# A hybrid decoder layer: attention without carried states, another order of the last steps, and eight unread products

## The chip, the cores and the metric

The kernel runs on one core of a Trainium2 chip. The metric is the time on the device in microseconds (us) of one execution, the median of several; less is better. The engines are named as the profile names them: PE is TensorE (PEld its weight loads), DVE is VectorE, ACT is ScalarE, POOL is GpSimd, SP is SyncE, whose queue issues nearly all loads.

## The reference, cut to what matters

One layer over 256 tokens of width 1024: a token mixer (gated linear attention, GLA, with 4 heads, and a short convolution beside it), then a mixture of 64 experts with two experts per token, then a norm. In chunks of 64 tokens the attention is

```python
b = jnp.cumsum(gc, axis=3)                  # gc: log of the forget gate, within a chunk
q_t = qc * jnp.exp(b)
k_t = kc * jnp.exp(-b)
k_s = kc * jnp.exp(b_last - b)
attn = jnp.where(causal, jnp.einsum('nbhid,nbhjd->nbhij', q_t, k_t), 0.0)
o_intra = jnp.einsum('nbhij,nbhjv->nbhiv', attn, vc)
def step(state, inp):                       # over the four chunks
    q_i, k_i, v_i, d_i = inp
    o_i = jnp.einsum('bhid,bhdv->bhiv', q_i, state)
    return d_i[..., None] * state + jnp.einsum('bhid,bhiv->bhdv', k_i, v_i), o_i
o = o_intra + o_inter                       # then a norm per head, silu(r), a projection
```

and the end of the layer

```python
x = x + g2 * hier_moe(h)        # each expert: (silu(x @ w1[e]) * (x @ w3[e])) @ w2[e]
return rmsnorm(x, final_norm_g)
```

Everything is fp32 with 476 MB of weights, most of them the experts'; all 64 experts are computed.

## The kernel before

**Loads.** `Stream` issues the weights from SP's queue. The projections' weights come in blocks of 128x1024 into a ring of 12 slots (`bfree`, L72); a slot is loaded again when `bdone` says that its block is used up. Whatever tiles the first part doesn't need any more become slots for units of 2 MB (128x4096, `free`, L107), 12 units for each of 16 groups of 4 experts. So a load starts when the engine that used the slot's last content is done.

**First part (to about 292 us).** The projection `h @ W_in` and the output projections go through `items`, blocks of 128 output columns (`mm_blk`, L356: 24 products, high and low part of the split fp32 operands). For each block ScalarE rounds the weights (`split_h`, L340) and VectorE takes the remainder (`split_l`, L347), five blocks ahead. VectorE also forms the modulation vectors from weights as they come (`mod_blk`, L257; table `MODS` says beside which block). All else is hung on a block's number: `first(b, f)` runs f ahead of that block's weight casts, `pre(b, f)` ahead of its `split_l`, `at(b, f)` just before its products. The engines work in the order written, so this sets what stands behind what.

**Attention in it.** `gate0` to `gate8` form the forget gate; `gate4` scans it within chunks of 64 (bb). `eb`, `enb` and `ekb` are exp(b), exp(-b), exp(b_last - b); `q_evac` and `k_evac` multiply them into q and k as these leave PSUM (qt, kt_, ks). `gla_kst` (L481) transposes ks, `gla_attn` (L494) forms 128x128 scores per head and half of the tokens, `gla_attn2` (L498) copies their causal part within chunks into `at`. `gla_state` (L506) forms k_s^T v for chunks 0, 1 and 2, `gla_state2` (L513, L515) decays and adds them. `gla_o` sums per head and half of the head's 256 value columns two products with `at` (L525) and three with the states (L529). `gla_ss` to `gla_ss4` form the norms; `gla_ss4` spreads the four rows of `scr2` over 128 partitions by products with the mostly zero `P1` (L556). PSUM tiles `m` come from four banks in turn (`mt`).

**Experts.** Per group of four experts: 8 units of the first layer (`l1_unit`, through `tile_mm`, L1048: four strips of 32 columns), `act` (silu, product, four transposes L1059, copy), 4 units of the second layer, `evac_y` (L1066: output weights into SBUF), and during the next group `combine` (L1075: back to the tokens, L1079: added to `total`).

**The end.** The last group's second layer is stored by output columns (`el`, `LASTC`: 512, 256, 128 and 128 columns), each of its units loaded in `LASTN` pieces. Each part goes through `last_mm` (L1200) and `last_part` (L1066, L1075, L1079, squares on L1214 and, for the last, on L1211); `last_weigh` (L1218) multiplies by the final gain. Then come the sum of squares (L1241), root, reciprocal, scaling and four stores (L1247 to L1252). The order is that of the code:

```python
last_mm(part 0) ; last_part(0)
last_mm(part 1) ; last_weigh(0) ; last_part(1)
last_mm(part 2) ; last_weigh(1) ; last_part(2)
last_mm(part 3) ; last_weigh(2) ; last_part(3, True)
```

Of the kernel before, what the change touches and what calls it, by code (L numbers as in the profile page):

```python
# [28 lines left out]
LASTN = (2, 2, 4, 4)  # L29
# [88 lines left out]
def trunk_kernel(ctx: ExitStack, tc: tile.TileContext, xT: bass.AP, c: bass.AP, modw: bass.AP,  # L118
# [113 lines left out]
    V.memset(cmask[0:64, 64:128], 0)  # L232
# [219 lines left out]
    def gate5():  # L452
        S.activation(eb, bb, AF.Exp, scale=-1.0 / 16)

    def gate6():
        V.tensor_sub(ekb.rearrange("p h (c t) -> p (h c) t", t=64),
                     b4[:, :, 63:64].to_broadcast([128, 16, 64]), b4)

    def gate7():
# [16 lines left out]
    def gla_kst():
        L["pk"] = []
        for tt in range(TT):
            ps = mt(H, 128)
            for h in range(H):  # L480
                T.transpose(ps[:, h], ks[:, h, 128 * tt:128 * tt + 128], ident)  # L481
            L["pk"].append(ps)

    def gla_kst2():
        for tt in range(TT):
            S.copy(L["kst"][:, tt], fl(L["pk"][tt]))

    def gla_attn():
        L["pa"] = []
        for tt in range(TT):  # L490
            s = slice(128 * tt, 128 * tt + 128)
            ps = mt(H, 128)
            for h in range(H):
                T.matmul(ps[:, h], kt_[:, h, s], qt[:, h, s], start=True, stop=True)  # L494
# [2 lines left out]
    def gla_attn2(tt):
        V.copy_predicated(L["at"][:, tt], cmask[:, None, :].to_broadcast([128, H, 128]), L["pa"][tt])  # L498

    def gla_state(*chs):  # L500
        for ch in chs:
            L["ps", ch] = [mt(2, 256) for _ in range(2)]
        for h in range(H):
            for ch in chs:
                tt, r = ch // 2, slice(64 * (ch % 2), 64 * (ch % 2) + 64)
                T.matmul(L["ps", ch][h // 2][:, h % 2], L["kst"][r, tt, 128 * h:128 * h + 128],  # L506
                         L["v"][r, tt, 256 * h:256 * h + 256], start=True, stop=True)

    def gla_state2(ch):
        new = L["S", ch + 1]  # L510
        for h in range(H):
            if ch == 0:
                S.copy(new[:, h], L["ps", ch][h // 2][:, h % 2])  # L513
            else:
                V.scalar_tensor_tensor(new[:, h], L["S", ch][:, h], decay[:, h, ch:ch + 1],  # L515
                                       L["ps", ch][h // 2][:, h % 2], op0=OP.mult, op1=OP.add)

    def gla_o(h):
        ps = mt(2, TOK)
        vt = L["v"]  # L520
        for a in range(2):
            f = 256 * h + 128 * a
            for tt in range(TT):
                s = slice(128 * tt, 128 * tt + 128)
                T.matmul(ps[:, a, s], vt[:, tt, f:f + 128], L["at"][:, tt, h],  # L525
                         start=(a == 0 and tt == 0), stop=False, skip_group_check=True)
            for ch in range(1, 4):
                s = slice(64 * ch, 64 * ch + 64)
                T.matmul(ps[:, a, s], L["S", ch][:, h, 128 * a:128 * a + 128], qt[:, h, s],  # L529
                         start=False, stop=(a == 1 and ch == 3), skip_group_check=True)  # L530
# [20 lines left out]
    def gla_ss4():  # L551
        L["rso"] = []
        for h in range(H):
            if h % 2 == 0:
# [1 line left out]
            T.matmul(L["rso"][h // 2][:, h % 2], P1[:, h // 2, h % 2], scr2, start=True, stop=True)  # L556
# [764 lines left out]
```

## Time and profile before

| what | value |
|---|---|
| time, median of 3 runs | 1206.16 us (1203.33 to 1206.17) |
| the profiled execution, its own time | 1202.4 us |
| its span in the profile | 1200.5 us |
| PE busy | 903.8 us (75%) |
| DVE busy | 381.6 us (32%) |
| ACT busy | 224.6 us (19%) |
| read from memory | 475.79 MB, 397 GB/s over the span |

The span is counted from the first to the last recorded event; the time of the execution is 1.9 us more. A busy share is a mean over stages that differ: the share of the whole says little about which engine another waits for at a given time. In the timeline a row is a start, a length, the engine, the code's line, the operation, the tile written and the tiles read, the size, a count, and in brackets the idle time ahead of it with what ended it.

### The profile page before, as it was taken

The page shows a single profiled execution, that of the slowest core. Times are in us where ns is not written, and L with a number is a line of the kernel's source. Part 1 is how long each engine was busy: PE and PEld are TensorE (multiplying, and loading weights), DVE is VectorE, ACT ScalarE, POOL GpSimd, SP SyncE. Part 2 cuts the span into 40 slices and gives each one's busy share as a digit, 9 for nine tenths or more (in the row PEclk, how much of TensorE's full clock was granted, in tenths as well). Part 3 has the DMA queues.
Part 4 walks back from the last instruction along what each step waited for, and adds up shares of the span by engine and source line. Part 5 has one row for each costly group of instructions (what it writes and reads, how often), then busy time and mean ns, then how long its engine had stood idle before and what let it go on. Part 6 is the DMA issues. An engine that isn't in the chain of part 4 may idle for free.

```text
span 1200.5 us, 14607 instructions
## 1 busy us (share of the span) xinstructions
PE 903.8 (75%) x6188; PEld 476.8 (40%) x6188; DVE 381.6 (32%) x720; ACT 224.6 (19%) x375; POOL 3.9 (0%) x15
## 2 busy tenths in 40 slices
PE   9999999999888766666666667676667566756575
PEld 6999999999342212121212212121212111412112
DVE  8968699664431111111111101020202000302103
ACT  6775545443210101010101000000000000100002
POOL 0000000000000000000000000000000000000000
PEclk9999999999998888798788888788888886989888
DMA  9987589979999999999999999999999999999996
GB/s 369 396 339 254 177 300 339 381 271 364 421 430 430 429 432 431 430 431 430 430 432 430 429 432 430 430 432 429 431 431 430 431 430 431 428 432 431 429 428 261
DMA packets 51483, 477.84 MB, mean 398 GB/s; under 512 B 5971, under 2 KB 6099, under 8 KB 27093
## 3 DMA queue, kind: packets, MB, share of 16 engines
q1 hardware_dynamic: 50544, 475.81, 95.8%
q8 instruction: 50, 0.82, 0.2%
q10 hardware_dynamic: 868, 1.05, 0.2%
q14 instruction: 21, 0.16, 0.0%
HBM read 475.79 MB, written 1.05 MB: 397 GB/s over the span
## 4 chain that ended last, share of the span: by engine, by line
DMA 67%; PE 28%; DVE 3%; ACT 0%; issue 0%; DVEq 0%; SPq 0%; ACTq 0%
DMA unit<-in_ew_dram 45%; DMA ring<-in_ew_dram 19%; PE z L356 17%; PE a L1048 3%; DMA unit<-in_el_dram 2%; PE m L364 2%; PE z L373 2%; PE m L1020 1%; PE m L1075 1%; PE m L529 0%; DMA xt<-in_xT_dram 0%; PE z L220 0%; PE m L506 0%; PE m L525 0%; PE m L312 0%
## 5 line engine op out<-in xcount | busy, mean ns | idle before, releaser
L1048 PE MATMUL a<-unit,xt 128*32 128x512 f32 x1440 | 209.5, 711 | 103.9 <-DMA unit<-in_ew_dram 103.9
L1048 PE MATMUL a<-unit,gt 128*32 128x512 f32 x736 | 121.7, 799 | 63.5 <-DMA unit<-in_ew_dram 59.9
L1048 PEld LDWEIGHTS a<-unit,xt 128*32 128x32 f32 x1440 | 43.8, 120 | 248.2 <-DMA unit<-in_ew_dram 139.0
L356 PE MATMUL z<-hhl,sp 128*128 128x256 f32 x1152 | 140.9, 284 | 0.0
L356 PEld LDWEIGHTS z<-hhl,sp 128*128 128x128 f32 x1152 | 138.9, 192 | 1.6 <-issue 1.5
L1024 ACT ACTIVATE xt<-m,modc,A 128x128 f32<-128x128 f32 x64 | 25.9, 453 | 518.5 <-PE m L1020 517.4
L347 DVE TENSOR_TENSOR sp<-ring,sp 128x1024 fp32r<-128x1024 f32 x88 | 106.8, 1219 | 40.2 <-ACT sp L340 40.1
L1048 PE MATMUL a<-ring,xt 128*32 128x512 f32 x608 | 84.2, 676 | 35.9 <-DMA ring<-in_ew_dram 35.9
L340 ACT CAST sp<-ring 128x1024 fp32r<-128x1024 f32 x88 | 91.5, 1048 | 93.8 <-PE z L356 66.6
L1079 DVE TENSOR_TENSOR wk<-wk,m 128x512 f32<-128x512 f32 (+2 forms) x64 | 41.7, 654 | 194.5 <-PE m L1075 194.5
L1066 DVE TENSOR_TENSOR xt<-a,xt 128x1024 f32<-128x1024 f32 (+3 forms) x19 | 20.0, 1054 | 257.4 <-PE a L1048 249.8
L1048 PEld LDWEIGHTS a<-unit,gt 128*32 128x32 f32 x736 | 24.3, 129 | 148.6 <-DMA unit<-in_ew_dram 93.1
L1075 PE MATMUL m<-xt,pwt 128*128 128x512 f32 (+2 forms) x136 | 64.5, 617 | 5.2 <-DVE xt L1066 5.2
L1056 DVE TENSOR_TENSOR gt<-gt,a 128x512 f32<-128x512 f32 x16 | 11.0, 687 | 173.8 <-ACT gt L1055 173.8
L1020 PEld LDWEIGHTS m<-scr,wk 128*128 128x128 f32 x512 | 58.7, 192 | 19.0 <-issue 18.7
L1020 PE MATMUL m<-scr,wk 128*128 128x128 f32 x512 | 62.4, 279 | 3.7 <-DVE scr L1009 2.9
L257 DVE SCALAR_TENSOR_TENSOR xt<-ring,xt 128x1024 f32<-128x1024 f32 x48 | 58.5, 1218 | 0.6 <-DMA ring<-in_modw_dram 0.2
L1048 PEld LDWEIGHTS a<-ring,xt 128*32 128x32 f32 x608 | 18.6, 117 | 97.3 <-DMA ring<-in_ew_dram 49.3
L1026 DVE TENSOR_SCALAR xt<-m,A,modc 128x128 f32<-128x128 f32 x64 | 23.3, 405 | 103.9 <-PE m L1020 103.9
L1048 PE MATMUL a<-ring,gt 128*32 128x512 f32 x208 | 36.3, 833 | 21.8 <-DMA ring<-in_ew_dram 21.1
L1075 PEld LDWEIGHTS m<-xt,pwt 128*128 128x128 f32 x136 | 26.0, 206 | 50.3 <-issue 38.0
L1055 ACT ACTIVATE gt<-a 128x512 f32<-128x512 f32 x16 | 9.6, 597 | 182.3 <-PE a L1048 182.3
(255 smaller groups left out, 633.0 us busy)
## 6 DMA issues: line engine op xcount, KB each, us to landing
unit<-in_ew_dram SPq DMA_DIRECT2D x136, 2048.0 KB, 38.8
ring<-in_ew_dram SPq DMA_DIRECT2D x48, 2048.0 KB, 38.8
ring<-in_win_dram SPq DMA_DIRECT2D x88, 512.0 KB, 7.8
ring<-in_modw_dram SPq DMA_DIRECT2D x48, 512.0 KB, 6.8
ring<-in_ew_dram SPq DMA_DIRECT2D x12, 512.0 KB, 7.3
unit<-in_el_dram SPq DMA_DIRECT2D x4, 1024.0 KB, 31.6
ring<-in_el_dram SPq DMA_DIRECT2D x4, 512.0 KB, 20.2
unit<-in_el_dram SPq DMA_DIRECT2D x4, 512.0 KB, 11.2
```

The source lines that it names most:

```text
L257: V.scalar_tensor_tensor(scr, st.block("m", i, b), 1.0, cB, op0=OP.mult, op1=OP.mult, accum_out=modc[:, 4 * i + b:4 * i + b + 1])
L340: S.copy(sp(b)[:, 0], st.block("w", n, i))
L347: V.tensor_sub(t[:, 1], st.block("w", n, i), t[:, 0].bitcast(F32))
L356: T.matmul(ps, t[:, ws, k], rhs[rs][:, k], start=(clear and k == 0 and n == 0), stop=(k == KT - 1 and n == 2), skip_group_check=True)
L364: T.matmul(pb[:, h % 2], t[:, ws, h], hl[rs][:, kk], start=(kk == 0 and h % 2 == 0 and n == 0), stop=(kk == KT - 1 and h % 2 == 1 and n == ...
L373: T.matmul(pv[tt][hh], hl[rs][:, kk, 128 * tt:128 * tt + 128], t[:, ws, 512 * hh:512 * hh + 512], start=(kk == 0 and n == 0), stop=(kk == ...
L1020: T.matmul(ps[j], acc[:, tt, f:f + 128], Pm[:, tt], start=(tt == 0), stop=(tt == 1))
L1024: S.activation(xg[:, k], ps[j], AF.Identity, bias=B2[:, k:k + 1], scale=A2[:, k:k + 1])
L1026: V.tensor_scalar(xg[:, k], ps[j], A2[:, k:k + 1], B2[:, k:k + 1], op0=OP.mult, op1=OP.add)
L1048: T.matmul(ps[32 * j:32 * j + 32, 512 * hh:512 * hh + 512], lhsT[:, 32 * j:32 * j + 32], w[:, j, 512 * hh:512 * hh + 512], start=first, st ...
L1075: T.matmul(ps[:, :w], pwt[:, tt], X["y"][:, s], start=True, stop=True)
L1079: V.tensor_add(total[:, tt, s], total[:, tt, s], ps[:, :w])
```

## The change

Three edits go together. Lines called L... in the rows below are of the kernel that the rows are of.

**1. Attention without states.** A half of 128 tokens is now scaled about its own middle: for keys, `ek` holds in a half's first chunk the decay from the token to that chunk's end (from `wE`), and in its second chunk the inverse of the decay since that chunk's start; for queries, `eq` is 1/`ek`. So a key times a later query of the same half has the decay between them, and needs no state (`kx`, `qx`). For the second half's queries against the first half's keys `gla_far` multiplies the keys by the decay over the second chunk and the queries by that over the third (`decay`; `kd`, `qd`). `gla_attn` forms near scores (128 columns for the first 64 keys, 64 for the other 64) and far ones, `gla_near` copies the causal part, `gla_cross` the far part, and `gla_o` needs two products per head and half: one over all 256 tokens, one over the last 128. `gla_kst`, `gla_state` and their evacuations are gone. `gla_ss4` spreads the norm rows with one row of ones each (K of 1, partitions 0, 32, 64, 96) into four PSUM tiles, so P1 need not be cleared. Three blocks of `MODS` change places.

**2. Another order at the end.** `last_part` is cut into `last_evac` and `last_sums`; part 3's products follow part 2's at once, parts 2 and 3 lie in another PSUM tile (`ps2`), the gains are multiplied in smaller steps, the final scaling of the last 256 columns takes the gain along, and five stores take the place of four. `LASTN` goes from (2, 2, 4, 4) to (1, 2, 2, 4).

**3. Unread products.** In the last group five products of ones (bf16, 512 columns) into a PSUM tile that nothing reads stand between the units u = 6 and u = 7 of the first layer (called unit 6 and unit 7 below), and three more ahead of the silu's transposes.

TensorE's order in the attention before (`z` are the projections' blocks, `m` the attention's PSUM tiles; the counts are the code's):

```order
L356 MATMUL z<-hhl,sp 128x256 x240
L481 MATMUL m<-ident,gb 128x128 x8
L356 MATMUL z<-hhl,sp 128x256 x24
L494 MATMUL m<-gb 128x128 x8
L356 MATMUL z<-hhl,sp 128x256 x24
L506 MATMUL m<-t_126,gc 128x256 x8
L356 MATMUL z<-hhl,sp 128x256 x48
L506 MATMUL m<-t_126,gc 128x256 x4
L356 MATMUL z<-hhl,sp 128x256 x48
L525 MATMUL m<-gc,t_126 128x128 x2
L529 MATMUL m<-gb,gc 128x64 x3
```

and after:

```order
L352 MATMUL z<-hhl,sp 128x256 x288
L487 MATMUL m<-gb 64x128
L488 MATMUL m<-gb 64x64
...
L485 MATMUL m<-gb 128x128 x4
L352 MATMUL z<-hhl,sp 128x256 x96
L505 MATMUL m<-gc,t_120 128x256
L506 MATMUL m<-gc,t_120 128x128
```

Transposes and states are gone; near scores (L487, L488, eight pairs) and far ones (L485) stand together, one block later than the scores before, and an output needs two products for five.

ScalarE's order at the gate's exponentials (`t_181`, `t_175` and `gb` are the gate tiles, L340 and L336 the casts for the splits) before:

```order
L340 CAST sp<-ring 128x1024
L453 ACT_TABLE_LOAD
L453 ACTIVATE t_181<-t_181 128x1024
L340 CAST sp<-ring 128x1024
L715 COPY t_126<-z 128x512
L463 ACTIVATE t_181<-t_181 128x1024
L464 ACTIVATE gb<-gb 128x1024
L340 CAST sp<-ring 128x1024 x2
L715 COPY t_126<-z 128x512
```

and after:

```order
L336 CAST sp<-ring 128x1024
L460 ACT_TABLE_LOAD
L460 ACTIVATE t_175<-gb 128x8x64
L461 ACTIVATE t_175<-t_175 128x8x64
L460 ACTIVATE t_175<-gb 128x8x64
L461 ACTIVATE t_175<-t_175 128x8x64
L463 ACTIVATE decay<-t_175 128x4 x2
L336 CAST sp<-ring 128x1024
L684 COPY t_120<-z 128x512
L336 CAST sp<-ring 128x1024 x2
L684 COPY t_120<-z 128x512
```

The one exponential ahead of the cast is now four of half the size and two of four columns; the two that stood behind the next copy are gone.

TensorE's order at the end before (L1048 the last group's first layer, L1200 the second layer's parts, L1075 the combining):

```order
L1048 MATMUL a<-unit,xt 32x512 x24
L1059 MATMUL m<-ident,gt 128x128 x4
L1200 MATMUL a<-unit,gt 32x512 x16
L1075 MATMUL m<-xt,pwt 128x512 x2
L1200 MATMUL a<-ring,gt 32x256 x16
L1075 MATMUL m<-xt,pwt 128x256 x2
L1200 MATMUL a<-unit,gt 32x128 x16
L1075 MATMUL m<-xt,pwt 128x128 x2
L1200 MATMUL a<-unit,gt 32x128 x16
L1075 MATMUL m<-xt,pwt 128x128 x2
```

and after, from unit 7 of the first layer on (L1016 is the first layer, L1182 the second, L1051 the combining; five unread products stand ahead of the first row):

```order
L1016 MATMUL a<-unit,xt 32x512 x8
L1026 LDWEIGHTS onesb
L1026 MATMUL m<-onesb 128x512
...
L1026 MATMUL m<-onesb 128x512
L1035 MATMUL m<-ident,gt 128x128 x4
L1182 MATMUL a<-unit,gt 32x512 x16
L1051 MATMUL m<-xt,pwt 128x512 x2
L1182 MATMUL a<-ring,gt 32x256 x16
L1051 MATMUL m<-xt,pwt 128x256 x2
L1182 MATMUL a<-unit,gt 32x128 x32
L1051 MATMUL m<-xt,pwt 128x128 x4
```

Three unread products stand ahead of the transposes, part 3's products have joined part 2's, and both are combined after them. In VectorE's order the evacuations of both (`last_evac`) accordingly stand ahead of the last four additions.

The diff, cut:

```diff
-LASTN = (2, 2, 4, 4)
+LASTN = (1, 2, 2, 4)
...
-MODS = (16, 17, 18, 19, 22, 26, 27, 28, 31, 33, ...
+MODS = (16, 17, 18, 19, 22, 26, 28, 29, 30, 33, ...
...
-    V.memset(cmask[0:64, 64:128], 0)
...
-    G.memset(P1, 0.0)
-    for h in range(H):
-        G.memset(P1[32 * h:32 * h + 1, h // 2, h % 2], 1.0)
...
+    wE, qx, kx = gb[:, 0, 0:2].rearrange("p h t -> p (h t)"), gb[:, 1], gb[:, 3]
...
+    def half(t, c):
+        return t.rearrange("p h (a c t) -> p (h a) c t", c=2, t=64)[:, :, c]
...
     def gate5():
-        S.activation(eb, bb, AF.Exp, scale=-1.0 / 16)
+        V.tensor_sub(wE, half(bb, 0)[:, :, 63:64].to_broadcast([128, 8, 64]), half(bb, 0))
     def gate6():
-        V.tensor_sub(ekb.rearrange("p h (c t) -> p (h c) t", t=64),
-                     b4[:, :, 63:64].to_broadcast([128, 16, 64]), b4)
-    def gate7():
-        V.tensor_copy(decay, eb.rearrange("p h (c t) -> p h c t", t=64)[:, :, :, 63])
-    def gate8():
-        S.activation(enb, bb, AF.Exp, scale=1.0 / 16)
-        S.activation(ekb, ekb, AF.Exp, scale=-1.0 / 16)
+        for d, sg in ((ek, -1.0), (eq, 1.0)):
+            S.activation(half(d, 0), wE, AF.Exp, scale=sg / 16)
+            S.activation(half(d, 1), half(bb, 1), AF.Exp, scale=-sg / 16)
+        for c in range(2):
+            S.activation(decay[:, c], bb[:, :, 64 * c + 127], AF.Exp, scale=-1.0 / 16)
...
+    def gla_far():
+        for d, x, c, o in ((kd, kx, 0, 0), (qd, qx, 1, 128)):
+            V.tensor_mul(d, x[:, :, o:o + 128], decay[:, c, :, None].to_broadcast([128, H, 128]))
...
     def gla_attn():
         L["pa"] = []
-        for tt in range(TT):
-            s = slice(128 * tt, 128 * tt + 128)
+        a, b = slice(0, 128), slice(128, 256)
+        for k, q in ((kx[:, :, a], qx[:, :, a]), (kx[:, :, b], qx[:, :, b]), (kd, qd)):
             ps = mt(H, 128)
             for h in range(H):
-                T.matmul(ps[:, h], kt_[:, h, s], qt[:, h, s], start=True, stop=True)
+                if k is kd:
+                    T.matmul(ps[:, h], k[:, h], q[:, h], start=True, stop=True)
+                    continue
+                T.matmul(ps[0:64, h], k[:, h, 0:64], q[:, h], ...)
+                T.matmul(ps[64:128, h, 64:128], k[:, h, 64:128], q[:, h, 64:128], ...)
             L["pa"].append(ps)
...
+    def gla_near(tt):
+        t, ps = (L["at0"][:, :, 0:128], L["at1"])[tt], L["pa"][tt]
+        for n, c in ((64, 0), (128, 64)):
+            V.copy_predicated(t[:n, :, c:c + 64], cmask[:n, None, c:c + 64]..., ps[:n, :, c:c + 64])
+    def gla_cross():
+        S.copy(L["at0"][:, :, 128:256], L["pa"][2])
     def gla_o(h):
...
+            T.matmul(ps[:, a], vt[:, 0, f:f + 128], L["at0"][:, h], start=(a == 0), ...)
+            T.matmul(ps[:, a, 128:256], vt[:, 1, f:f + 128], L["at1"][:, h], ...)
...
     def gla_ss4():
-        L["rso"] = []
+        L["rso"] = [mt(TOK) for _ in range(H)]
         for h in range(H):
-            if h % 2 == 0:
-                L["rso"].append(mt(2, TOK))
-            T.matmul(L["rso"][h // 2][:, h % 2], P1[:, h // 2, h % 2], scr2, start=True, stop=True)
+            r = slice(32 * h, 32 * h + 1)
+            T.matmul(L["rso"][h], onesf[r], scr2[r], start=True, stop=True)
...
-    at(21, gate6)
-    first(22, gate5)
-    first(23, gate8)
-    at(23, gate7)
+    at(21, gate5)
+    first(22, gate6)
...
+    at(27, gla_far)
-    at(27, gla_kst)
-    at(28, gla_attn)
-    first(28, gla_kst2)
-    pre(29, gla_attn2, 0)
-    pre(29, gla_attn2, 1)
-    at(29, gla_state, 0, 1)
-    first(30, gla_state2, 0)
-    pre(30, gla_state2, 1)
-    at(31, gla_state, 2)
-    pre(32, gla_state2, 2)
+    at(29, gla_attn)
+    first(31, gla_cross)
+    pre(31, gla_near, 0)
+    pre(31, gla_near, 1)
...
     def k_evac(j):
-        V.tensor_mul(ks[:, s], pk[j], ekb[:, s])
-        V.tensor_mul(kt_[:, s], pk[j], enb[:, s])
+        V.tensor_mul(kx[:, s], pk[j], ek[:, s])
...
+    def unread(n):
+        p = mt()
+        for _ in range(n):
+            T.matmul(p, onesb, onesb[:, None, :].to_broadcast([128, 4, 128]), start=True, stop=True)
-    def act(ps):
+    def act(ps, fill=0):
+        if fill:
+            unread(fill)
         S.activation(gt, ps[:, 0:512], AF.Silu)
...
             l1_unit(ps, g, u, unit("e", g, u))
+            if g == last and u == 6:
+                unread(5)
...
-        act(ps)
+        act(ps, 3 if g == last else 0)
...
-    last_weigh(0)
-    last_part(1)
+    last_evac(1)
+    last_weigh(0, 512, 0, 1)
+    last_sums(1)
+    last_weigh(0, 512, 1, 2)
...
-    for f in range(4):
-        last_mm(768, 128, w[:, 0, f], f)
-    last_weigh(1)
-    last_part(2)
-    for f in range(4):
-        last_mm(896, 128, w[:, 1, f], f)
-    last_weigh(2)
-    last_part(3, True)
+    for n in (2, 3):
+        for f in range(4):
+            last_mm(n, w[:, n - 2, f], f)
+        if n == 2:
+            last_evac(2)
+    last_weigh(512, 256)
+    last_evac(3)
+    last_sums(2)
+    last_sums(3)
...
+    put(V, nc.sync, 0, 0, 512)
+    put(S, S, 1, 0, 512)
+    put(V, nc.sync, 0, 512, 1024)
+    put(S, S, 1, 512, 768)
+    put(V, nc.sync, 1, 768, 1024)
```

More of the change, by code (lines that the diff above doesn't have):

```diff
@@ L411, in trunk_kernel @@
     L["o"] = gb[:, 2:4].rearrange("p a h t -> p (a h) t")
-    ekb, qt, kt_, ks = (gb[:, i] for i in range(4))
-    decay = sm.tile([128, H, 4], F32, name="decay")
-    b4 = bb.rearrange("p h (c t) -> p (h c) t", t=64)
+    wE, qx, kx = gb[:, 0, 0:2].rearrange("p h t -> p (h t)"), gb[:, 1], gb[:, 3]
+    wE = wE.rearrange("p (a t) -> p a t", t=64)
+    kd, qd = (gb[:, 2].rearrange("p h t -> p (h t)")[:, 512 * i:512 * i + 512].rearrange("p (h t) -> p h t", h=H)
+              for i in range(2))
+    decay = sm.tile([128, 4, H], F32, name="decay")
+    def half(t, c):
+        return t.rearrange("p h (a c t) -> p (h a) c t", c=2, t=64)[:, :, c]
     def gate0():
@@ L497, in gla_attn2 @@
[L497 to L507, printed above, removed]
@@ L522, in gla_o @@
             f = 256 * h + 128 * a
[L523 to L530, printed above, removed]
+            T.matmul(ps[:, a], vt[:, 0, f:f + 128], L["at0"][:, h], start=(a == 0), stop=False, skip_group_check=True)
+            T.matmul(ps[:, a, 128:256], vt[:, 1, f:f + 128], L["at1"][:, h], start=False, stop=(a == 1),
+                     skip_group_check=True)
         L["po", h] = ps
@@ L1195, in trunk_kernel, with last_mm, last_evac, last_sums @@
     S.activation(dum, epsc, AF.Sqrt)
-    def last_mm(c0, cw, w, f):
+    ps2 = pa.tile([128, D], F32, name="a")
+    LASTP = (ps[:, 0:512], ps[:, 512:768], ps2[:, 0:128], ps2[:, 512:640])
+    sq1 = X["xg"][(last + 1) % 2].rearrange("p k s -> p (k s)")
+    def last_mm(n, w, f):
         for j in range(EPG):
-            T.matmul(ps[32 * j:32 * j + 32, c0:c0 + cw], gT[:, f, 32 * j:32 * j + 32], w[:, j],
+            T.matmul(LASTP[n][32 * j:32 * j + 32], gT[:, f, 32 * j:32 * j + 32], w[:, j],
                      start=(f == 0), stop=(f == 3), skip_group_check=True)
-    def last_part(n, tail=False):
+    def last_evac(n):
+        s = slice(LASTC[n][0], sum(LASTC[n]))
+        V.tensor_mul(X["y"][:, s], LASTP[n], X["g2r"][:, s])
+    def last_sums(n):
         c0, cw = LASTC[n]
-        evac_y(ps, c0, c0 + cw)
         combine(last, c0, c0 + cw)
@@ L1248, in trunk_kernel, with put @@
[L1248 to L1252 removed]
+    def put(e, q, tt, c0, c1):
+        t, r = total[:, tt, c0:c1], rs[:, tt:tt + 1]
+        if e is S:
+            S.activation(t, t, AF.Copy, scale=r)
+        elif c0 == 768:
+            V.scalar_tensor_tensor(t, t, r, fgr[:, c0:c1], op0=OP.mult, op1=OP.mult)
+        else:
+            V.tensor_scalar(t, t, r, None, op0=OP.mult)
+        q.dma_start(out[128 * tt:128 * tt + 128, c0:c1], t)
```

70 lines of the change are left out of this document (24 added, 46 removed).

## The prediction

> **What bounds the kernel now.** I read the page's slices first, then the busy time in stretches of 10 us, then the chain of waits, and last the timeline where the change stands. What the DMA moved in each slice of 30 us, and the chain's shares by engine:
>
> ```profile
> GB/s 369 396 339 254 177 300 339 381 271 364 421 430 430 429 432 431 430 431 430 430 432 430 429 432 430 430 432 429 431 431 430 431 430 431 428 432 431 429 428 261
> ...
> DMA 67%; PE 28%; DVE 3%; ACT 0%; issue 0%; DVEq 0%; SPq 0%; ACTq 0%
> ```
>
> From the twelfth slice on the DMA moves about 430 GB/s without a break: the expert weights. Before that it falls as low as 177. The stretches tell why (busy us of TensorE, its weight load, VectorE, ScalarE, GpSimd, with counts; granted clock; DMA share; GB/s):
>
> ```profile
> 120.00:130.00 10.00, 10.00 (x90) 10.00 (x89) 4.07 (x6) 4.26 (x6) 0.00 (x0) 1.00 0.51 161
> ...
> 310.00:320.00 10.00, 10.00 (x92) 3.46 (x88) 3.12 (x16) 5.12 (x13) 0.00 (x0) 1.00 1.01 429
> ```
>
> At 120 us TensorE (PE) is busy for the whole stretch and the DMA for half of it: buffers come free only as fast as TensorE uses them up. At 310 us it is the DMA that is full. The chain of waits (start, length, what) joins the two:
>
> ```profile
> 368.88 5.38 PE a L1048 x32
> 374.28 37.96 DMA unit<-in_ew_dram
> ...
> 1179.98 1.11 PE a L1200 x8
> ```
>
> So there are three stages. Up to 374.28 us the chain is mostly TensorE; from there the stream of weights runs for its own length, until 1179.98; then a ladder of short steps ends the program. A microsecond saved on TensorE in the first stage frees each later buffer a microsecond earlier and moves the whole stream. Engine time saved between 374 and 1180 us is worth nothing. The ladder counts one for one.
>
> **The attention: what goes.** TensorE's timeline of before (start, length; an fp32 product is recorded as two passes, so counts are twice the code's):
>
> ```profile
> 94.59 1.04 PE L481 MATMUL m<-ident,gb 128*128 128x128 f32 x8
> 95.38 3.11 PE L356 MATMUL z<-hhl,sp 128*128 128x256 f32 x24
> 98.33 1.95 PE L494 MATMUL m<-gb 128*128 128x128 f32 x16
> 100.04 3.11 PE L356 MATMUL z<-hhl,sp 128*128 128x256 f32 x24
> 103.08 0.70 PE L506 MATMUL m<-t,gc 64*128 64x256 f32 x2
> 104.86 1.99 PE L506 MATMUL m<-t,gc 64*128 64x256 f32 x14 [1.08 <-DVE gc L498]
> 106.78 6.02 PE L356 MATMUL z<-hhl,sp 128*128 128x256 f32 x48
> 112.73 1.99 PE L506 MATMUL m<-t,gc 64*128 64x256 f32 x8
> 114.65 6.01 PE L356 MATMUL z<-hhl,sp 128*128 128x256 f32 x48
> 120.50 0.61 PE L525 MATMUL m<-gc,t 128*128 128x128 f32 x4
> 120.94 0.78 PE L529 MATMUL m<-gb,gc 128*128 128x64 f32 x6
> ...
> 124.88 3.12 PE L356 MATMUL z<-hhl,sp 128*128 128x256 f32 x24
> ...
> 148.10 1.97 PE L556 MATMUL m<-scr,P 128*128 128x256 f32 x8
> 149.71 2.50 PE L356 MATMUL z<-hhl,sp 128*128 128x256 f32 x18
> ```
>
> From start to start: the transposes of k (L481) 95.38 - 94.59 = 0.8 us; the scores (L494) 1.7; the states of chunks 0 and 1 (L506) 106.78 - 103.08 = 3.7, of which 1.08 is a wait for VectorE; chunk 2's 1.9; the outputs of heads 0 and 1 (L525, L529) 124.88 - 120.50 = 4.4, of heads 2 and 3 the same again; spreading the norms (L556) 1.6. Together 18.5 us.
>
> **What comes.** Far scores: four products of 128x128, half of L494: 0.85.
>
> Near scores: eight products of 128 and eight of 64 columns, in the two column halves of the array. One after the other they take 16 passes at L494's 0.107 and 16 at L529's: an output quarter is 4.38 / 4 = 1.1, of which L525 is 0.44 (0.11 a pass), which leaves 0.11 for each of six. That is 3.5. But strips can overlap, as in the gate's first product:
>
> ```profile
> 60.10 1.07 PE L420 MATMUL z<-t,e 128*32 128x256 f32 x16
> ```
>
> Sixteen passes of 256 columns in 1.07 are 0.067 each, against 0.24 for L506's (1.92 / 8). If the shorter half disappears under the longer one, 1.7 is left. I take 2.2, nearer to the row with strips.
>
> Outputs: per head and half now one product of 256 and one of 128 columns. Passes of 256 took 0.20 (1.61 / 8, L556) to 0.24, passes of 128 0.11. Eight times two of each: 5.0 to 5.6; I take 5.4.
>
> Norms: four products of one row, each in a row strip of its own. One after the other 1.6; overlapped as L506's two row halves (14 passes in 1.92, 0.137 each, against 0.24) 0.9; with four strips at best 0.5. I take 1.0.
>
> Sum 9.45, bounds 8.05 and 11.55. The stage gets 18.5 - 9.45, about **9.0 us**, shorter (7.0 to 10.5).
>
> **What could wait there.** ScalarE's gate exponentials move ahead of a weight cast (L340), and with it of VectorE's split (L347):
>
> ```profile
> 85.57 1.03 ACT L340 CAST sp<-ring 128x1024 fp32r<-128x1024 f32 x1
> ...
> 86.63 1.22 DVE L347 TENSOR_TENSOR sp<-ring,sp 128x1024 fp32r<-128x1024 f32 x1 [1.14 <-ACT sp L340]
> ...
> 106.43 1.65 DVE L515 SCALAR_TENSOR_TENSOR gc<-gc,decay,m 128x256 f32<-128x256 f32 x4
> ```
>
> One exponential stood ahead of that cast; now four of half the size (about 0.55, half of the cast's) and two tiny ones do, some 2.7 us for 1.06, and they begin 0.4 later, when VectorE's subtraction is done. The cast then starts near 87.7, the split near 88.7, 2 us late. But VectorE has less to do: the second multiplication of k, half of the subtraction and the eight state updates (twice 1.65) go, two far multiplications and two more masked copies come. Counting its queue on from 88.7, the far multiplications end near 101.8; TensorE, 0.8 us earlier than before, reaches the far scores near 94.6 + 2 x 2.95 + 2.2 = 102.7. I cost that at nothing; the other end is 2 us. The cover for the late cast, and for the three modulation blocks that change places (a VectorE pass each, and their loads in SP's queue), is how far splits run ahead of TensorE:
>
> ```profile
> 150.76 1.22 DVE L347 TENSOR_TENSOR sp<-ring,sp 128x1024 fp32r<-128x1024 f32 x1
> ...
> 180.59 1.22 DVE L347 TENSOR_TENSOR sp<-ring,sp 128x1024 fp32r<-128x1024 f32 x1
> ```
>
> The first of these is for the block that TensorE takes up sixth after 149.71 (2.9 each: about 164 us), the last, nine splits on, for that of about 190, 8 us ahead; that is the least in the stretch. P1's and the mask's clearing at the start lie beside the first loads: nothing.
>
> **The unread products.** Five go ahead of unit 7 of the last group, three into the pause for silu. The nearest row is the start's L220, of the same shape:
>
> ```profile
> 11.93 3.29 PE L220 MATMUL z<-onesb 128*128 128x512 bf16 x8
> ...
> 1165.30 3.46 PE L1048 MATMUL a<-unit,xt 128*32 128x512 f32 x16 [2.26 <-DMA unit<-in_ew_dram]
> 1170.17 1.92 PE L1048 MATMUL a<-unit,xt 128*32 128x512 f32 x16 [1.41 <-DMA unit<-in_ew_dram]
> ...
> 1179.98 1.06 PE L1200 MATMUL a<-unit,gt 128*32 128x512 f32 x8 [0.58 <-DMA unit<-in_el_dram]
> ```
>
> Eight took 3.29 us: five 2.1, three 1.2. Unit 6 ends at 1168.76, so its pause is 1.4, and unit 7 comes at most 0.7 late; the three lie beside silu and its multiplication. All this is ahead of 1179.98, where TensorE waits 0.58 for the DMA: nothing, or 0.5 if the cold pace holds. What they can bring is the clock (the column after GpSimd):
>
> ```profile
> 1176.00:1178.00 2.00, 2.00 (x12) 0.37 (x8) 0.00 (x0) 0.37 (x2) 0.00 (x0) 0.50 1.04 432
> ...
> 1182.00:1184.00 2.00, 2.00 (x8) 0.70 (x12) 0.80 (x2) 0.25 (x1) 0.00 (x0) 1.00 0.91 373
> ```
>
> It was halved ahead of the ladder and full inside it: nothing to gain in this execution. The Trainium skill, "TensorE: Matmul & The Clock Gate", HAM oscillation, says that an idle window of about 3.4 us drops the clock to half. The rows agree as to the halving; by the rule the sum stays, since the ladder is at full clock with the eight and without.
>
> **The ladder.** Its last rounds, and the end of the stream:
>
> ```profile
> 1189.92 0.28 DVE L1066 TENSOR_TENSOR xt<-a,xt 128x128 f32<-128x128 f32 x1
> ...
> 1190.26 0.71 PE L1075 MATMUL m<-xt,pwt 128*128 128x128 f32 x4 [1.08 <-DVE xt L1066]
> ...
> 1190.90 1.08 PE L1200 MATMUL a<-unit,gt 128*32 128x128 f32 x32
> ...
> 1192.32 0.28 DVE L1066 TENSOR_TENSOR xt<-a,xt 128x128 f32<-128x128 f32 x1
> ...
> 1194.27 0.16 DVE L1241 TENSOR_REDUCE rs<-ssq 128x2 f32<-128x8 f32 x1
> ```
>
> ```profile
> 1189.80:1190.00 0.20, 0.00 (x0) 0.00 (x0) 0.20 (x2) 0.00 (x0) 0.00 (x0) 1.00 0.00 0
> ```
>
> A round of evacuation, combining, adding and squaring takes 2.4 us (1192.32 - 1189.92), and part 3's products (1190.90) stand behind part 2's combining on TensorE although nothing more was to land after 1189.8. Now they follow part 2's products. Their second half starts at 1189.8 and takes 0.54; from the start of the last evacuation to the reduction it was 1194.27 - 1192.32 = 1.95. That gives 1192.3 and, since part 2's combining (0.64) now stands ahead of part 3's and lies only partly beside the evacuation, 1192.4: **1.9 us** earlier. Weights that land a little before 1189.8 give up to 2.6; a combining and two squares wholly in the way leave 0.5. The scaling at the end is five stores for four, the last ones smaller: nothing, 0.2 either way. Fewer, larger pieces of the last units change when a first half may start, not when the last lands: nothing.
>
> **Sum.** 9.0 + 1.9 = 10.9. The profiled execution took 1202.4 us (span 1200.5), which gives 1191.5. The three timed runs lie at 1203.33 to 1206.17, median 1206.16, 3.8 above it. From the mean of the four, 1204.5, I say 1193.6, rounded to 1194.
>
> **Rivals.** First: small products are dear (14 in 100). After L506's products of half height the next weight load idles 0.33 us:
>
> ```profile
> 106.78 5.81 PEld L356 LDWEIGHTS z<-hhl,sp 128*128 128x128 f32 x48 [0.33 <-issue]
> ```
>
> If every change of strip cost that, near scores and norms would be 20 x 0.33 = 6.6 us dearer: gain 4.3, about 1200. Against it: L506's 14 passes change halves without such a gap. The Trainium skill, "TensorEngine Tiling (Array Packing)", Key Properties, says that a change of tiling mode drains TensorE, not one of tile; by that, this case doesn't arise.
>
> Second: the stream doesn't follow (8 in 100). If the DMA already bounds the first stage, only the ladder's 1.9 stays: 1202.6, no difference to be told. For it: the DMA is full from 310 on, ahead of the handover at 374.28. Against it: its share of 0.51 at 120 us, time in which it can take up what is asked for earlier.
>
> Third: slower (4 in 100). VectorE becomes the bound after 150 us, where its splits come out of an unbroken row of work. If its queue lags by more than the 8 us ahead, each further microsecond is one of TensorE's; from 8 + 11 + 4 = 23 us of lag on, the kernel is over 0.3% slower, and at 25 us near 1209. The lag that I count is 2 us.
>
> The forecast has 74 in 100. Faster by over 0.3% (3.6 us, about what a measurement here can tell from no change): 74 + 14 = 88; within 0.3%: 8; slower: 4. The range goes from 1188 (10.5 + 2.6 off the profiled run, and one more) to 1201 (7.0 - 2 + 0.5 = 5.5 off the median), which takes in the first rival.
>
> **What would show it.** TensorE: near and far scores about 3.1 us, outputs 5.4, norms 1.0, no wait at the far scores. The handover to the stream near 365.3 instead of 374.28, the ladder's first wait near 1171 instead of 1179.98, and from it to the reduction 12.4 us instead of 14.3, at a clock of 1.00. I am wrong if blocks between 94 and 150 us wait for VectorE, if strips don't overlap, or if the handover moves and the end of the stream doesn't.

## The result, and the profile after

The changed kernel took 1191.57 us (median; 1191.09 to 1193.16), the kernel before, beside it on the same chip, 1204.91 (1203.33 to 1206.17): a ratio of 0.9892, 95% interval 0.9874 to 0.991. Run again later it took 1191.98 against 1204.03: 0.9903 (0.9888 to 0.9918). The profiled execution took 1191.67 us, 10.7 less than that of before, with a span of 1189.0, 11.5 less. The forecast was 1194, a gain of 10.9 in profiled time.

The slices of 30 us, and the chain's shares by engine:

```profile
GB/s 370 397 339 290 214 321 380 330 286 402 423 429 430 430 430 431 431 430 430 431 430 431 430 432 429 430 431 430 430 431 431 430 430 430 428 430 430 432 430 272
...
DMA 70%; PE 28%; DVE 1%; ACT 0%; issue 0%; ACTq 0%; SPq 0%; DVEq 0%
```

The plateau of 430 GB/s stands as it did. What rose is the dip ahead of it: 214 in the fifth slice for 177, 402 in the tenth for 364; only the eighth fell, 330 for 381. The same bytes are asked for earlier. The stretch at 120 us says the same (columns as in the prediction):

```profile
120.00:130.00 10.00, 10.00 (x86) 9.07 (x85) 6.45 (x10) 6.64 (x10) 0.00 (x0) 1.00 0.62 194
```

TensorE's timeline in the attention:

```profile
100.02 0.32 PE L487 MATMUL m<-gb 128*64 128x128 f32 x1
100.03 0.33 PE L488 MATMUL m<-gb 128*64 128x64 f32 x2
...
101.60 0.38 PE L487 MATMUL m<-gb 128*64 128x128 f32 x2
101.92 1.16 PE L485 MATMUL m<-gb 128*128 128x128 f32 x8
102.83 11.76 PE L352 MATMUL z<-hhl,sp 128*128 128x256 f32 x96
114.42 0.60 PE L505 MATMUL m<-gc,t 128*128 128x256 f32 x2
...
116.96 3.12 PE L352 MATMUL z<-hhl,sp 128*128 128x256 f32 x24
119.92 0.60 PE L505 MATMUL m<-gc,t 128*128 128x256 f32 x2
...
122.45 1.80 PE L352 MATMUL z<-hhl,sp 128*128 128x256 f32 x13
...
138.33 0.71 PE L532 MATMUL m<-scr,onesf 1*128 1x256 f32 x8
138.97 3.25 PE L352 MATMUL z<-hhl,sp 128*128 128x256 f32 x25
```

From start to start: near scores (L487, L488) 1.90 us, far scores (L485) 0.91, outputs (L505, L506) 2.54 and 2.53, norms (L532) 0.64; 8.5 in all, for 18.5 before. No row has idle time ahead of it in brackets. The block behind the norms begins at 138.97, and began at 149.71: 10.7 us.

The end, TensorE's rows first, then VectorE's, then ScalarE's:

```profile
1157.07 1.25 PE L1026 MATMUL m<-onesb 128*128 128x512 bf16 x5
1160.07 1.92 PE L1016 MATMUL a<-unit,xt 128*32 128x512 f32 x16 [1.74 <-DMA unit<-in_ew_dram]
1161.93 0.82 PE L1026 MATMUL m<-onesb 128*128 128x512 bf16 x3
...
1169.88 1.06 PE L1182 MATMUL a<-unit,gt 128*32 128x512 f32 x8 [1.40 <-DMA unit<-in_el_dram]
...
1178.95 1.42 PE L1182 MATMUL a<-unit,gt 128*32 128x128 f32 x32 [0.41 <-DVE xt L1187]
1180.30 1.19 PE L1051 MATMUL m<-xt,pwt 128*128 128x128 f32 x8
```

```profile
1180.44 0.29 DVE L1187 TENSOR_TENSOR xt<-a,xt 128x128 f32<-128x128 f32 x1 [0.95 <-PE a L1182]
...
1182.31 0.16 DVE L1230 TENSOR_REDUCE rs<-ssq 128x2 f32<-128x8 f32 x1 [0.15 <-ACT wk L1199]
```

```profile
1183.03 0.72 ACT L1238 ACTIVATE wk<-wk,rs 128x512 f32<-128x512 f32 x1 [0.23 <-DVE rs L1233]
1183.79 0.38 ACTq L1243 DMA_DIRECT2D out_dram<-wk  x1
1184.21 0.51 ACT L1238 ACTIVATE wk<-wk,rs 128x256 f32<-128x256 f32 x1 [0.46 <-ACT wk L1238]
1184.75 0.35 ACTq L1243 DMA_DIRECT2D out_dram<-wk  x1
```

The last wait for a large piece of weights ends at 1169.88 (1179.98 before: 10.1 earlier). From there to the reduction it takes 12.43 us, 14.29 before. Parts 2 and 3 are now multiplied in one run (L1182 x32 twice, L1051 x8), and one evacuation, one run of additions and a square lie behind. From the reduction to the end of the span it is 6.7 us, for 6.2: ScalarE scales and stores twice in a row, and its last issue comes at 1184.75, 2.4 after the reduction; before, its one issue came at 1195.74, 1.5 after it (experiment 4 shows that this doesn't account for the 0.5):

```profile
1195.74 0.38 ACTq L1249 DMA_DIRECT2D out_dram<-wk  x1
```

So 10.1 + 1.9 - 0.5 = 11.5, the whole difference of the spans.

### The profile page after: what moved, and what is told of

Same layout as the page of the kernel before. It is cut to its first block, busy times and chain, and to the rows that moved or that the text cites. A ratio compares the mean times of both kernels' runs of the same rounds, so it can differ in the third digit from the quotient of the medians.

```text
span 1189.0 us, 14492 instructions
## 1 busy us (share of the span) xinstructions
PE 896.9 (75%) x6140; PEld 468.8 (39%) x6140; DVE 376.7 (32%) x712; ACT 222.7 (19%) x374; POOL 2.8 (0%) x11
## 4 chain that ended last, share of the span: by engine, by line
DMA 70%; PE 28%; DVE 1%; ACT 0%; issue 0%; ACTq 0%; SPq 0%; DVEq 0%
DMA unit<-in_ew_dram 46%; DMA ring<-in_ew_dram 19%; PE z L352 18%; DMA unit<-in_el_dram 4%; PE a L1016 3%; PE m L360 2%; PE z L369 2%; PE m L988 1%; PE z L220 0%; PE m L1051 0%; PE m L292 0%; PE m L505 0%; PE m L308 0%; PE m L654 0%; DMA e<-in_c_dram 0%
## 5 line engine op out<-in xcount | busy, mean ns | idle before, releaser
L1016 PE MATMUL a<-unit,xt 128*32 128x512 f32 x1440 | 211.4, 718 | 92.0 <-DMA unit<-in_ew_dram 91.9
L1016 PE MATMUL a<-unit,gt 128*32 128x512 f32 x736 | 121.1, 794 | 67.2 <-DMA unit<-in_ew_dram 65.0
L1016 PEld LDWEIGHTS a<-unit,xt 128*32 128x32 f32 x1440 | 44.4, 121 | 239.6 <-DMA unit<-in_ew_dram 126.2
L1016 PE MATMUL a<-ring,xt 128*32 128x512 f32 x608 | 86.9, 695 | 37.4 <-DMA ring<-in_ew_dram 37.4
L336 ACT CAST sp<-ring 128x1024 fp32r<-128x1024 f32 x88 | 91.4, 1048 | 87.7 <-PE z L352 67.0
L1042 DVE TENSOR_TENSOR xt<-a,xt 128x1024 f32<-128x1024 f32 x15 | 18.4, 1224 | 252.2 <-PE a L1016 252.2
L1016 PEld LDWEIGHTS a<-unit,gt 128*32 128x32 f32 x736 | 24.2, 129 | 151.8 <-DMA unit<-in_ew_dram 96.3
L1051 PE MATMUL m<-xt,pwt 128*128 128x512 f32 (+2 forms) x136 | 65.3, 625 | 2.7 <-DVE xt L1187 1.4
L1016 PEld LDWEIGHTS a<-ring,xt 128*32 128x32 f32 x608 | 19.0, 121 | 100.6 <-issue 50.3
L1016 PE MATMUL a<-ring,gt 128*32 128x512 f32 x208 | 34.4, 792 | 24.2 <-DMA ring<-in_ew_dram 23.5
L1051 PEld LDWEIGHTS m<-xt,pwt 128*128 128x128 f32 x136 | 26.5, 210 | 49.2 <-issue 40.0
```

What stands on the lines that cost most here:

```text
L336: S.copy(sp(b)[:, 0], st.block("w", n, i))
L1016: T.matmul(ps[32 * j:32 * j + 32, 512 * hh:512 * hh + 512], lhsT[:, 32 * j:32 * j + 32], w[:, j, 512 * hh:512 * hh + 512], start=first, st ...
L1051: T.matmul(ps[:, :w], pwt[:, tt], X["y"][:, s], start=True, stop=True)
```

## Experiments

Every kernel was timed in five rounds beside the kernel before. Theory: the time comes from the attention by way of TensorE, to which the stream of weights is tied one for one, and some 2 us from the end; the unread products bring nothing.

**1. The change in its parts.** Four kernels: the attention alone (with `MODS` and the clearings), the end alone, the whole change without unread products, and the unread products alone.

```diff
 # end alone, and whole without unread products
-            if g == last and u == 6:
-                unread(5)
...
-        act(ps, 3 if g == last else 0)
+        act(ps)
```

> Only the attention part of the change (with its clearing and modulation blocks); the end as before, no unread products. If the stream of weights follows TensorE one for one: TensorE reaches the block behind the norms 10.7 us earlier, as in the changed kernel (149.71 to 138.97), and the time falls by 10 to 11 us, to 0.991 of before. Rival, the stream follows only in part and the end and the clock carry the rest: 6 us or less, 0.995 or above.

> Only the new order at the end with its pieces and stores. Theory: from the ladder's first wait to the reduction 12.4 us instead of 14.3, the part behind the reduction 0.4 to 0.5 longer for the fifth store; time 1.4 us less, 0.9988. Rival, the end carries what the timed runs gained beyond the forecast (13.3 against 10.9): 3.5 to 4 us less, 0.997.

> The changed kernel without the eight unread products. Theory: the ladder's TensorE work on the chain is short and the last weights set its middle, so the time is that of the changed kernel within 1 us (0.989), even if the profile shows a clock below 1.00 ahead of the ladder. Rival, the products hold the clock where it counts: 2 to 4 us longer than the changed kernel, 0.991 to 0.992, with a clock of 0.50 in some stretch of the ladder.

> Before with the eight unread products and nothing else. Theory: 0 to 0.5 us less, not to be told from before (0.9995 to 1.0); the stretch ahead of the ladder (0.50 before) runs at a clock of 1.00. Rival, before's slower runs have a halved clock in the ladder: 2 to 3 us less, 0.998.

| kernel | median us | ratio to before (1203.62), 95% interval |
|---|---|---|
| attention alone | 1193.75 | 0.9914 (0.9901 to 0.9927) |
| end alone | 1202.5 | 0.9991 (0.9982 to 1.0) |
| whole, without unread products | 1191.82 | 0.9898 (0.9883 to 0.9912) |
| unread products alone | 1203.61 | 1.0005 (0.9996 to 1.0014) |

The attention brings 9.9 us. The end brings 1.1 alone and 1.9 on top of the attention; these two differ by less than two such runs can tell. The unread products alone bring nothing that shows, and the whole change without them is as fast as with them. A second pair was to tell a gain of half a microsecond from none:

> The changed kernel once more, as the partner of the others of this group: 11 to 13 us less than before, 0.989 to 0.991.

> The changed kernel without the unread products, beside the changed kernel on the same chip. The first profile without them had a clock of 0.50 through the ladder's first step and a reduction 0.7 us later. Theory now: they are worth 0.5 to 1 us here. Rival (the forecast): nothing, within 0.3 us of its partner. Second rival: 2 us or more.

It gave 1191.98 (0.9903; 0.9888 to 0.9918) with them and 1192.33 (0.9903; 0.9888 to 0.9918) without. The four runs with them alone spread over 2 us (1190.86 to 1192.91), so half a microsecond is neither shown nor excluded. What they do to the clock is visible all the same. Busy time in stretches of the first of the kernels without them, and its reduction:

```profile
1164.00:1166.00 2.00, 1.17 (x8) 0.77 (x12) 0.05 (x1) 0.67 (x2) 0.00 (x0) 0.50 1.01 426
...
1168.00:1170.00 2.00, 2.00 (x12) 0.40 (x8) 0.00 (x0) 0.00 (x0) 0.00 (x0) 0.50 1.02 422
...
1178.00:1180.00 2.00, 1.59 (x35) 0.99 (x34) 1.79 (x5) 1.02 (x4) 0.00 (x0) 1.00 0.09 37
...
1183.02 0.16 DVE L1228 TENSOR_REDUCE rs<-ssq 128x2 f32<-128x8 f32 x1 [0.15 <-ACT wk L1197]
```

and of the changed kernel:

```profile
1164.00:1166.00 2.00, 1.03 (x13) 0.42 (x16) 0.00 (x0) 1.80 (x2) 0.00 (x0) 1.00 1.01 426
1168.00:1170.00 2.00, 0.60 (x12) 0.12 (x8) 0.00 (x0) 0.00 (x0) 0.00 (x0) 1.00 1.03 422
```

TensorE's clock is 0.50 there without the unread products and 1.00 with them, and part 0's products take all of the time instead of a part of it. But the DMA share behind the clock is 1.0 in those stretches either way, so nothing says that the last pieces land sooner for it, and the clock is back at 1.00 before they are used. The reduction comes 0.7 later in this execution (1183.02 for 1182.31). When the changed kernel was run again, it came at 1182.88, so two executions of one kernel differ there by nearly as much.

**2. Does the stream follow TensorE?** This separates the forecast from its second rival. 24 unread products go onto TensorE of the changed kernel, once ahead of block 60 of the first part and once inside the stream.

```diff
+    def idle_products():
+        p = mt()
+        for _ in range(24):
+            T.matmul(p, onesb, onesb[:, None, :].to_broadcast([128, 4, 128]), start=True, stop=True)
+    at(60, idle_products)
 # the other kernel
+            if g == 8 and u == 5:
+                unread(24)
```

> The changed kernel with 24 unread products of 512 columns (about 0.22 us each at full clock, 5.2 us) on TensorE ahead of block 60 of the first part. If the stream of weights follows TensorE one for one: 4 to 5.5 us slower than the changed kernel, 1196 to 1197.5 us. If the DMA already bounds the first part there (the second rival of the prediction): no difference, about 1192.

> The changed kernel with the same 24 unread products on TensorE inside the stream, in group 8 behind unit 5. If TensorE's time is worth nothing there, no difference: 1191.5 to 1192.3 us. If a late buffer costs the stream time there too, 2 to 5 us slower.

TensorE's rows, in the first kernel and then in the second:

```profile
200.57 5.35 PE L581 MATMUL m<-onesb 128*128 128x512 bf16 x24
205.57 11.87 PE L352 MATMUL z<-hhl,sp 128*128 128x256 f32 x96
...
1175.41 1.07 PE L1188 MATMUL a<-unit,gt 128*32 128x512 f32 x8 [1.39 <-DMA unit<-in_el_dram]
```

```profile
743.75 5.35 PE L1026 MATMUL m<-onesb 128*128 128x512 bf16 x24
```

In the first part 5.0 us of products (205.57 - 200.57) cost 5.6: 1196.72 us (0.9948; 0.9934 to 0.9961) against 1191.13 (0.9901; 0.9886 to 0.9916) with the same products in the stream, which is no more than the changed kernel takes. The wait for the large piece ends at 1175.41 instead of 1169.88, 5.5 later. In this execution TensorE was 1.0 us behind already ahead of the products (139.95 for 138.97 at the block behind the norms), so 6.0 us of lateness arrive there as 5.5, which is within what two executions differ by. So a microsecond of TensorE is worth about one microsecond in the first part and none at the one place in the stream that was tried. The second rival is out.

**3. How much can VectorE lag?** The third rival, and the cover of 8 us that the prediction read from how far the splits run ahead. Extra VectorE passes go ahead of block 40 of the changed kernel, 12 in one kernel and 4 in another (the count in `range`).

```diff
+    def idle_passes():
+        for _ in range(12):
+            V.tensor_mul(scr, cB, cB)
+    at(40, idle_passes)
```

> The changed kernel with 12 multiplications of 128x1024 more on VectorE (its own scratch, read by nothing), 1.2 us each, 14.5 us together, at block 40, ahead of the stretch where VectorE works without pause. If splits run 8 us ahead where it is least, TensorE waits for what is over: 6 us more than its partner, 1197 to 1199. Rival, VectorE has idle time behind that takes it up: 0 to 1 us more. Rival, it was the bound already: 13 to 15 us more.

> The changed kernel with 4 extra VectorE passes (5.0 us) ahead of block 40, where 12 passes (15.1 us) had cost 15.9 us. If the 8 us by which the splits run ahead were a cover, no difference: about 1192 us. If VectorE has next to no slack there, as the 12 passes suggest, about 5 us slower, 1196 to 1198; if part of it is covered and TensorE's clock fell with the 12 because it waited for several us in a row, 1 to 3 us slower.

With 12 (15.1 us) the time is 1207.84 (1.0037; 1.0023 to 1.005), 15.9 above the changed kernel beside it; with 4 (5.0 us) 1198.22 (0.9956; 0.9943 to 0.997), 6 to 7 above the changed kernel's 1191.1 to 1192.0. So in the time nothing was covered. VectorE's row with 12, and TensorE's:

```profile
145.07 15.08 DVE L580 TENSOR_TENSOR xt<-xt 128x1024 f32<-128x1024 f32 x12
```

```profile
164.68 8.47 PE L352 MATMUL z<-hhl,sp 128*128 128x256 f32 x46 [4.99 <-DVE sp L343]
179.63 5.60 PE L352 MATMUL z<-hhl,sp 128*128 128x256 f32 x27 [6.49 <-DVE gb L704]
```

With 4, TensorE's rows, then the evacuation on VectorE, then the stretches with the clock:

```profile
139.38 26.17 PE L352 MATMUL z<-hhl,sp 128*128 128x256 f32 x216
169.91 48.66 PE L352 MATMUL z<-hhl,sp 128*128 128x256 f32 x384 [4.36 <-DVE gb L704]
218.40 11.80 PE L352 MATMUL z<-ohl,sp 128*128 128x256 f32 x97
...
1178.83 1.94 PE L1187 MATMUL a<-unit,gt 128*32 128x512 f32 x8 [2.59 <-DMA unit<-in_el_dram]
```

```profile
169.08 0.68 DVE L704 TENSOR_TENSOR gb<-gb,z 128x512 f32<-128x512 f32 x1
```

```profile
166.00:168.00 2.00, 0.00 (x0) 0.00 (x0) 2.00 (x4) 1.56 (x2) 0.00 (x0) 1.00 0.77 217
168.00:170.00 2.00, 0.09 (x1) 0.12 (x1) 2.00 (x5) 0.00 (x0) 0.00 (x0) 0.61 0.82 289
170.00:172.00 2.00, 2.00 (x10) 2.00 (x11) 1.96 (x4) 0.00 (x0) 0.00 (x0) 0.50 0.80 270
172.00:174.00 2.00, 2.00 (x11) 2.00 (x11) 2.00 (x4) 1.55 (x3) 0.00 (x0) 0.50 0.84 277
```

For comparison, the same evacuation when the changed kernel was run again (its block behind the norms began at 139.03), and the first of the blocks of `ohl` in the changed kernel's first profile:

```profile
163.80 0.69 DVE L699 TENSOR_TENSOR gb<-gb,z 128x512 f32<-128x512 f32 x1
```

```profile
211.10 23.20 PE L352 MATMUL z<-ohl,sp 128*128 128x256 f32 x192
```

Two things show. First, what TensorE waited for with 4 passes isn't a split. It is the evacuation of a finished block's PSUM tile (`b_evac`, L704), which stands in VectorE's queue too; it came 5.3 us later (169.08 for 163.80) and TensorE waited 4.36. TensorE itself was 0.35 late by then (139.38 for 139.03), so the slack there is about 0.6 us (5.3 - 4.36 - 0.35), an estimate from these rows. With 12 passes the splits' cover ran out as well: two waits, 5.0 and 6.5 us. Second, the wait costs more than itself. After it TensorE ran at half clock for some 5 us, and the blocks of `ohl` begin 7.3 us later than in the changed kernel (218.40 - 211.10), of which 0.4 stood ahead of the passes: 6.9 for a wait of 4.36. The Trainium skill, "TensorE: Matmul & The Clock Gate", HAM oscillation, has it that an idle window of about 3.4 us halves TensorE's clock. The trace agrees as to the halving, not quite as to the time: TensorE is idle from 165.55 (169.91 - 4.36), and a mean of 0.61 from 168 to 170 puts the fall from 1.00 to 0.50 near 168.4, 2.9 us later, an estimate.

This profiled execution took 1201.99 us, the other four 1197.06 to 1198.67. What it has on top stands at the end: its last wait for a large piece is 2.59 us long instead of 1.40 and ends 9.0 later than in the changed kernel, and TensorE runs at half clock behind it, in spite of the unread products (the combining of part 0 takes 3.78 us for 1.98). From that wait to the reduction, at 1193.48, it takes 14.65 us for 12.43. So half clock in the middle of the ladder cost some 2 us here, and the passes themselves are better judged by the median.

**4. A further step at the end.** Part 2 is combined between the halves of part 3's products, and ScalarE's two last stores become one of 768 columns.

```diff
+    last_evac(2)
     last_weigh(512, 256)
+    for f in range(2):
+        last_mm(3, w[:, 1, f], f)
+    last_sums(2)
+    for f in range(2, 4):
+        last_mm(3, w[:, 1, f], f)
...
-    put(S, S, 1, 0, 512)
+    put(S, S, 1, 0, 768)
...
-    put(S, S, 1, 512, 768)
```

> The changed kernel with part 2 combined between the two halves of part 3's products, and with ScalarE's two last stores made one of 768 columns (four stores again). Theory: from the last landing to the reduction 0.4 us less (TensorE waits there now), from the reduction to the end of the span 6.2 to 6.4 us instead of 6.7: together 0.7 us less than its partner. Rival: the landing moves or the larger store lands later: no difference.

1192.23 us (0.9906; 0.9892 to 0.9919), against 1191.98 for the changed kernel beside it: no difference, so the 0.7 expected isn't there, or is below what five rounds tell. The profile shows neither half of it. From the last wait for a large piece (1169.62) to the reduction (1182.50) it takes 12.9 us for 12.43: TensorE combines part 2 (1179.33) ahead of the second half of part 3's products (1179.97), and the last evacuation (1180.68) stands 11.1 us behind that wait for 10.6. From the reduction to the end of the span it takes 6.6 us, where 6.2 to 6.4 was expected: ScalarE's one issue comes at 1184.19, 1.7 after the reduction for 2.4, but the stores now land 2.8 to 3.2 us after their issue, and in the kernel before it was 2.1 to 3.0. No version was faster than the changed kernel by more than these runs can tell.

## Why the prediction was right

**The mechanism held.** The saving on TensorE in the first part went through the whole stream: 10.7 us behind the norms, 10.1 at the last wait for a large piece, 9.9 in the time of the attention alone. Experiment 2 shows the tie with another cause on the same engine. The 0.6 between 10.7 and 10.1 is hardly more than two executions of one kernel differ by: the two profiles of the changed kernel reach the block behind the norms at 138.97 and 139.03, and the last wait ends at 1169.88 and 1170.36.

**The terms of the attention.** Each product was 0 to 0.4 us cheaper than I took it, the far scores excepted: near scores 1.90 (said 2.2), far 0.91 (0.85), outputs 5.07 (5.4), norms 0.64 (1.0); together 8.5 for 9.45. Near scores lay close to the bound of full overlap, 1.7: an L487 pass starts every 0.11 us and the L488 passes of 64 columns lie under them. Four row strips of one row each took 0.64, nearer to the bound of 0.5 than to the 0.9 of two halves. So the gain was 10.0 instead of 9.0 here. The other 0.7 of the 10.7 came from places that the sum didn't have. The near scores begin at 100.02, where 94.59 and two blocks of 2.95 make 100.5; 0.4 of this stands ahead of the attention already (a long row of blocks begins at 65.20, and at 65.61 before), and need not be the change's, for with the same first part two other profiles came to the block behind the norms 1.0 later (139.95 and 140.05). And the four blocks from 102.83 to 114.42 take 11.6, where 106.78 to 112.73 and 114.65 to 120.50 make 11.8, with a switch to the states between them.

**No drain (the first rival).** A pair of L487 and L488 changes column halves twice, and a pair starts every 0.11 us, without a gap of 0.33. Between the last pair and the far scores, a change of the array's shape, the weight load idles 0.17:

```profile
101.50 0.25 PEld L487 LDWEIGHTS m<-gb 128*64 128x64 f32 x2
101.91 0.97 PEld L485 LDWEIGHTS m<-gb 128*128 128x128 f32 x8 [0.17 <-DVE sp L343]
```

The Trainium skill, "TensorEngine Tiling (Array Packing)", Key Properties, says that a change of mode drains TensorE, not one of tile; the trace agrees as to the pairs. At changes of shape the weight load did idle: 0.17 us here, 0.23 ahead of the norms' products and 0.33 behind them, so the gap that the rival priced was there, but not at each strip. (The split named as the releaser is not an operand of L485; the multiplication that is one ended earlier, below.)

**The late cast.** VectorE's far multiplications were expected to end near 101.8, TensorE to get there near 102.7:

```profile
99.43 1.28 DVE L476 TENSOR_TENSOR gb<-gb,decay 128x512 f32<-128x512 f32 x2
```

They ended at 100.7, and TensorE came at 101.9. Nothing waited, as costed.

**The step that was wrong without harm** is the cover: "how far splits run ahead of TensorE", 8 us as the least in the stretch. It looked at one product of VectorE's queue alone. The first thing to be missed was another one, the PSUM tile's evacuation, with about 0.6 us to spare in the changed kernel. It did no harm because the change itself does not delay VectorE there: no row of TensorE behind the attention shows a wait for it. But the third rival's price was far off: the prediction put the point from which the kernel is over 0.3% slower at 23 us of lag. The runs put 5.0 us of lag at a cost of 6 to 7 and 15.1 at 15.9; from these two, as an estimate, break-even with the gain is near 11, and over 0.3% slower near 15. The chance of 4 in 100 rested on a margin that wasn't there.

**The unread products.** Their price was taken at the cold pace, 3.3 us for eight; they took 1.25 + 0.82 = 2.1, at full clock. Unit 7 was not late: it waited 1.74 for its weights. That they bring nothing held, as far as these runs can tell. The reason given, a ladder already at full clock, held for that execution; in the end alone the ladder's first steps ran at 0.50, which the prediction did not have as a case:

```profile
1178.00:1180.00 2.00, 2.00 (x12) 0.40 (x8) 0.00 (x0) 0.96 (x2) 0.00 (x0) 0.50 1.00 422
```

**The ladder.** From the first wait to the reduction 12.43 us, said 12.4. Its wait of 0.41 for VectorE ahead of part 3's products wasn't in the sum, and cost nothing: the last piece landed later still, at 1179.73 by the weight load's own wait. After the reduction "nothing, 0.2 either way" was mis-sized: 0.5 more. ScalarE's second scaling and issue stand there, but with one issue instead of two experiment 4 still took 0.4 more than before, so the cause stays open.

**A sign that was no sign.** "The handover to the stream near 365.3 instead of 374.28" did not come: the chain of waits leaves TensorE at 342.05.

```profile
342.05 36.42 DMA ring<-in_ew_dram
...
690.47 3.30 PE a L1016 x16
...
1164.94 14.74 DMA unit<-in_el_dram
```

Further on it even comes back to TensorE, for ten microseconds in which the DMA's share was 1.01. Each load in the stream waits for a buffer and for the queue ahead of it, so the chain may leave TensorE at any of several buffers that came free nearly in time. That makes the place a choice among near ties, not a time that shifts with the work ahead. The start of a fixed block (211.10 for those of `ohl`) or the last wait in the stream is the better mark.

**The level.** The profiled time was forecast as 1191.5 and came as 1191.67. That it fits so well is luck in part: by the spans the attention brought 10.1 for 9.0 and the end 1.4 for 1.9, and the time outside the span was 2.7 us for 1.9. The medians differ by 13.3 in the first comparison and by 12.05 when the changed kernel was run again. The 1194 came from adding the kernel's mean of four times, and lies within the same few microseconds by which the medians of before themselves move (1203.3 to 1206.2).

## What to carry to other kernels

Find the stage in which one engine sets when buffers come free; there its time is worth about one for one even where the DMA's total looks like the bound, and the same time in the next stage was worth nothing (5.6 us against none, for the same 24 products). A cover is the least over all that the engine does for the one that waits: splits were 8 us ahead and an evacuation some 0.6, so look at the PSUM tiles as well as at the operands. A stall on TensorE can cost more than its length: here 4.4 us cost 6.9, since some 5 us at half clock followed.

## What the runs showed of the hardware

Passes in the two column halves of the array overlap nearly fully: 16 fp32 passes of 128 columns and 16 of 64 took 1.90 us, 0.12 for each pair. Four row strips with one row each ran eight passes of 256 columns in 0.64 us, where the full array took 1.6. With eight unread bf16 products of 512 columns, 2.1 us of work, TensorE's clock stood at 1.00 from unit 7 to the reduction in seven of eight profiles; the exception is the one with 4 passes on VectorE, where a wait of 2.59 us came between. In the five profiles without them it was 0.50 for a part of that stretch. The time of the kernel did not change by as much as could be measured. Without them the clock fell there at pauses shorter than the 3.4 us of the Trainium skill's rule ("TensorE: Matmul & The Clock Gate", HAM oscillation); TensorE's last units in the first of the kernels without unread products:

```profile
1155.17 1.93 PE L1016 MATMUL a<-unit,xt 128*32 128x512 f32 x16 [1.64 <-DMA unit<-in_ew_dram]
1160.02 2.66 PE L1016 MATMUL a<-unit,xt 128*32 128x512 f32 x16 [2.93 <-DMA unit<-in_ew_dram]
```

The longest idle time is 2.93 us, and the unit behind it takes 2.66 us for 1.93: half clock for a part of it. Here the measurement is not what the rule would give.
